# The first layer's opening by feature tiles: sums, modulation and float32 products of two projection chunks in one loop over k

## The chip, the cores and the metric

The kernel runs as one program on one core of a Trainium2 chip. The metric is the device time of one execution in microseconds, taken from the median of several runs. Engines are named as in the profile: PE is TensorE (its weight loads are PEld), DVE is VectorE, ACT is ScalarE, POOL is GpSimd, and SP issues nearly all transfers. The core has 16 DMA engines.

## The reference, cut to what matters

Two layers run one after the other over 256 tokens of 1,024 features. What the change touches is the beginning of the first layer: the adaLN sums of shift and scale, the modulated input `h`, and the first 1,024 of the 7,680 columns of the combined projection (`q_a` and `k_a`, the queries and keys of the differential attention, which are rotated afterwards).

```python
c_act = jax.nn.silu(c)
for l in range(DEPTH):
    mod = c_act @ ada_w[l] + ada_b[l]
    shift_m, scale_m, gate_m, shift_f, scale_f, gate_f = jnp.split(mod[:, None, :], 6, axis=-1)
    h = rms_norm(x, mix_norm_g[l]) * (1.0 + scale_m) + shift_m
    y = hybrid_mixer(h, w_in[l], ...)      # z = h @ w_in, three attentions, gates, w_out
    x = x + gate_m * y
    h = rms_norm(x, ffn_norm_g[l]) * (1.0 + scale_f) + shift_f
    x = x + gate_f * hier_moe(h, ...)      # 32 experts, all their weights are read
return rms_norm(x, final_norm_g)
```

## The kernel before, in words

**Layout.** Features lie on partitions in eight tiles k = 0 to 7 (`KD`), tokens along the free dimension, so the transposed input `xT` is 128 x 8 x 256. All weights are read once, in float32, into a pool of ten `pair` buffers of 2 MB; half a pair is a `slot` of 1 MB. The framework's scheduler puts the instructions of each engine into an order of its own; only what is wrapped in `keep_in_program_order` stays where it is written. Each engine then works strictly through its list. Of SP's transfers eight are under way at most: each waits for the landing of the one eight places ahead of it.

**Projection.** `mixer` treats `w_in` as 15 chunks of 512 columns. `load` brings a chunk in as two slots. `gemm` takes it in four pieces of two feature tiles. `split` (L302, L303) cuts each piece into a rounded part `whi` (ScalarE) and a rest `wlo` (VectorE), and the input is cut in the same way into `hi` and `lo`; three products in the one-pass format fp32r then stand for one float32 product. Chunks 0 and 1 (`rq` and `rk` in the table `SEGS`) take 96 matmuls of 256 columns each. What a chunk leaves in PSUM (`z`, buffers `acc`, four of them) is put off in `pending` and written out in the middle of the next chunk: `place` copies the rotated halves (L461, four ScalarE copies of 32 partitions), multiplies with cosine and sine (L462, L463, VectorE) and adds the two (L464, GpSimd).

**The opening.** `run` issues eight `ada_part` first: 1 MB of `ada_w` each, two dot products with the conditioning row `grb` each (`ada_sum`, L166, VectorE), all of shift (section 0) and then all of scale (section 1). `first_loads` stands behind the second of them and brings in `k1` (identity), the small columns and `x`. `mixer` then squares `x` for the norm (L218), transposes it (L233), and `modulated` makes 1/rms (`rstd`, `rsqrt`), spreads it over partitions through TensorE as `R`, and goes over k: split of a piece of chunk 0, scaling (L263), shift to `hi` on ScalarE (L265), rest to `lo` (L257). Every k needs the finished sums of all 16 tiles, because `ada_done` (L175, L181) works on whole columns.

**Filling.** The other adaLN sections are summed in between: `FILL[l][n]` says how many 1 MB pieces are taken up ahead of chunk n.

**After the mixer's projections** come the three attentions interleaved with the gate chunks, `w_proj`, `w_out`, then `moe`, which streams the experts' weights through the ten pairs. Layer 1 goes the same way.

Of the kernel before, what the change touches and what calls it, by code (L numbers as in the profile page):

```python
# [53 lines left out]
def bc(ap, at, n):  # L54

    a = [list(e) for e in ap.ap]
    a.insert(at, [0, n])
    return bass.AP(tensor=ap.tensor, offset=ap.offset, ap=a)


class Kernel:
# [56 lines left out]

    def first_loads(self):
        nc, io = self.nc, self.io  # L120
        nc.sync.dma_start(self.k1, io["k1"])
        for l in range(DEPTH):
            nc.sync.dma_start(self.gcol[l], self.io["g_col"][l])
            nc.sync.dma_start(self.mcol[l], self.io["ada_b"][l])
        nc.sync.dma_start(self.x, io["x"].rearrange("(p t) d -> p t d", t=2))
        tri = self.rwg.rearrange("p k n -> p (k n)")[:, :P]
        nc.sync.dma_start(tri, io["tri"])
        nc.vector.tensor_copy(self.tri, tri)
# [34 lines left out]
            self.ada_done(l, s)  # L163

    def ada_sum(self, w, to):
        self.nc.vector.tensor_tensor_reduce(w, w, self.grb, scale=1.0, scalar=0.0, op0=OP.mult, op1=OP.add,  # L166
                                            accum_out=to)

    FILL = (0, 1, 0, 3, 0, 2, 2, 3, 2, 2, 3, 2, 3, 0, 1), (0, 0, 2, 2, 2, 2, 2, 2, 1, 3, 0, 0, 0, 0, 0)
    MOVED = (2, 3, 4, 5)  # L170

    def ada_done(self, l, s):
# [71 lines left out]
    def modulated(self, l, w):  # L244
# [24 lines left out]
        low(KD - 1)  # L269
        return hi, lo, parts  # L270

    def to_hilo(self, src, done):
# [77 lines left out]
    def mixer(self, l, fill):  # L350
# [15 lines left out]
        w0 = load(0)  # L366
        M = self.xT.rearrange("p k n -> p (k n)")

        def take(n, of):
# [1 line left out]
            for b in tiles:  # L371
                nc.gpsimd.memset(b[:, 2047:2048], 0.0)
            return tiles
        G2, Q0, Q1, K0, K1, V0, V1, T0, T1 = take(9, "long")
        self.homes = [self.slot("parts"), self.slot("parts"), None, None]
        ga = []
        tok = [M[:, t * D:(t + 1) * D] for t in range(2)]
# [16 lines left out]
            return T[:, o + 512 * i:o + 512 * (i + 1)]  # L394
        self.work, self.junk = work, T0[:, 1536:1664]

        if l == 0:
            self.new_sums()
            for t in range(2):
                for half in range(2):  # L400
                    hs = slice(half * 512, (half + 1) * 512)
                    self.square(t, half, self.x[:, t, hs], (T0, T1)[t][:, hs])
            for c in range(4):
                self.raw_t(c)
        hi, lo, halves = self.modulated(l, [w0[k // 4][:, k % 4:k % 4 + 2] for k in range(0, KD, 2)])
# [10 lines left out]

        def chunk(n):
            w = load(n) if n else w0
            if n == 0:
                nc.sync.dma_start(self.rope, io["rope"])  # L420
            if n == 1 and l:
                self.conditioning()
            if n == 4:
                late_loads()
            for _ in range(self.FILL[l][n]):
                if fill:
                    fill.pop(0)()
            evac, prods = [], []
            for kind, c0, wd, dst in SEGS[n]:
                if wd == 512:  # L430
                    z = [self.acc(), self.acc()]
                    prods += self.wide(z)
                    evac += [lambda t=t, z=z, kind=kind, dst=dst:
                             nc.scalar.copy(vdst[kind][:, t, dst:dst + 512], z[t]) for t in range(2)]
                    continue
                z = self.acc()
                if kind in vdst:
                    prods += [(z[:, t * 256:(t + 1) * 256], False, t, slice(c0, c0 + 256), t == 0) for t in range(2)]
                    evac.append(lambda z=z, kind=kind, dst=dst: nc.scalar.copy(
                        vdst[kind][:, :, dst:dst + 256], z.rearrange("p (t n) -> p t n", t=2)))  # L440
                    continue
                prods += self.flipped(z, c0)
                if kind == "g":
                    evac.append(lambda z=z, dst=dst: nc.scalar.activation(ga[dst // 2], z, AF.Tanh, scale=0.5))
# [18 lines left out]
            nc.vector.tensor_mul(v(sh), v(sh), sin)  # L463
            nc.gpsimd.tensor_add(d, d, sh)  # L464

        for n in range(9):
            chunk(n)
        self.flush()
        self.diff_attention(l, qT, kT, va, tok)
# [536 lines left out]
    def run(self):  # L1006
        self.setup()
        ada = lambda l, s: [lambda h=h: self.ada_part(l, s, h) for h in range(4)]
        for i, f in enumerate(ada(0, 0) + ada(0, 1)):
            if i == 2:  # L1010
                self.first_loads()
            f()
        fill = [[f for l, s in parts for f in ada(l, s)] for parts in (
            [(0, s) for s in (2, 3, 4, 5)] + [(1, s) for s in range(6) if s not in self.MOVED],
            [(1, s) for s in self.MOVED])]
        for l in range(DEPTH):
            self.mixer(l, fill[l])
            self.moe(l)
        self.final()


def layout(inputs):
# [88 lines left out]
```

## Time and profile before

| what | value |
|---|---|
| median of 3 runs | 1509.85 us (1509.48 to 1510.61) |
| the profiled execution's own time | 1507.89 us |
| its span, first to last instruction | 1506.0 us |
| mean granted TensorE clock | 0.907 of full speed |
| first layer: mixer, then experts | up to about 340 us, then up to about 800 us |
| bytes moved | 544.43 MB, mean 362 GB/s |

To read it: the page gives busy times over the span and in 40 slices of 37.65 us; the tables by stretch give the same for any window; the timeline lists single instructions with the idle time ahead of them and what ended it. A float32 matmul of the program stands as two MATMUL rows in the trace, an fp32r matmul as one. A duration of a MATMUL contains its modelled way through the array, so the pace is read from the distance between starts.

### The profile page before, as it was taken

The page shows a single profiled execution, that of the slowest core. Times are in us where ns is not written, and L with a number is a line of the kernel's source. Part 1 is how long each engine was busy: PE and PEld are TensorE (multiplying, and loading weights), DVE is VectorE, ACT ScalarE, POOL GpSimd, SP SyncE. Part 2 cuts the span into 40 slices and gives each one's busy share as a digit, 9 for nine tenths or more (in the row PEclk, how much of TensorE's full clock was granted, in tenths as well). Part 3 has the DMA queues.
Part 4 walks back from the last instruction along what each step waited for, and adds up shares of the span by engine and source line. Part 5 has one row for each costly group of instructions (what it writes and reads, how often), then busy time and mean ns, then how long its engine had stood idle before and what let it go on. Part 6 is the DMA issues. An engine that isn't in the chain of part 4 may idle for free. (4 is left out here: it accounts for less than half of the span.)

```text
span 1506.0 us, 19652 instructions
## 1 busy us (share of the span) xinstructions
PE 1198.5 (80%) x8146; PEld 787.0 (52%) x8146; DVE 614.6 (41%) x1246; ACT 372.2 (25%) x664; POOL 57.5 (4%) x67
## 2 busy tenths in 40 slices
PE   2999998989877676676778999999787578577675
PEld 2898987874333132231358989889443133133132
DVE  6889974572121021110149997457322112022012
ACT  2765554350000000000046656544100000000001
POOL 0102000100000000000001110010000000000001
PEclk7999998899988897897999999999998888798898
DMA  9887971769999999999996965276999999999997
GB/s 373 351 348 279 380 293 57 298 254 390 427 428 427 427 427 428 429 427 428 424 416 280 390 276 221 113 284 247 365 426 429 426 430 426 427 429 427 429 428 296
DMA packets 53084, 544.43 MB, mean 362 GB/s; under 512 B 7168, under 2 KB 8192, under 8 KB 12160
## 3 DMA queue, kind: packets, MB, share of 16 engines
q1 hardware_dynamic: 52992, 543.13, 86.9%
q8 instruction: 66, 1.08, 0.3%
q14 instruction: 26, 0.21, 0.0%
HBM read 542.04 MB, written 1.06 MB: 361 GB/s over the span
## 5 line engine op out<-in xcount | busy, mean ns | idle before, releaser
L95 PE MATMUL acc<-rg,xg 128*32 128x512 f32 x2048 | 282.0, 694 | 115.6 <-DMA rg<-w 113.5
L95 PE MATMUL acc<-rg,b 128*32 128x512 f32 (+1 forms) x1152 | 153.0, 662 | 95.9 <-DMA rg<-w2g 69.2
L95 PEld LDWEIGHTS acc<-rg,xg 128*32 128x32 f32 x2048 | 68.6, 119 | 304.3 <-issue 295.1
L95 PE MATMUL acc<-hi,wlo 128*128 128x256 f32 x704 | 200.2, 289 | 7.9 <-DVE wlo L303 7.7
L95 PE MATMUL acc<-lo,whi 128*128 128x256 f32 x704 | 196.1, 284 | 0.0
L95 PE MATMUL acc<-hi,whi 128*128 128x256 f32 x704 | 191.4, 286 | 1.2 <-ACT whi L302 1.1
L303 DVE TENSOR_TENSOR wlo<-rg,whi 128x1024 fp32r<-128x1024 f32 x116 | 145.0, 1250 | 59.1 <-ACT whi L302 58.1
L813 DVE TENSOR_TENSOR b<-b,acc 128x512 f32<-128x512 f32 x16 | 11.0, 688 | 353.1 <-PE acc L95 353.1
L302 ACT CAST whi<-rg 128x1024 fp32r<-128x1024 f32 x116 | 121.5, 1047 | 107.4 <-PE acc L95 99.2
L95 PEld LDWEIGHTS acc<-hi,wlo 128*128 128x128 f32 x704 | 135.1, 192 | 15.3 <-DVE wlo L303 11.6
L95 PEld LDWEIGHTS acc<-rg,b 128*32 128x32 f32 x1152 | 33.9, 120 | 197.1 <-DMA rg<-w2g 105.1
L95 PEld LDWEIGHTS acc<-lo,whi 128*128 128x128 f32 x704 | 134.5, 192 | 1.4 <-issue 1.0
L95 PEld LDWEIGHTS misc<-b,xn 128*128 128x128 f32 x512 | 124.6, 334 | 16.9 <-issue 15.5
L95 PEld LDWEIGHTS acc<-hi,whi 128*128 128x128 f32 x704 | 131.0, 192 | 2.9 <-ACT whi L302 2.1
L95 PE MATMUL misc<-b,xn 128*128 128x128 f32 x512 | 125.6, 404 | 3.9 <-DVEq L918 2.0
L166 DVE CUSTOM_DVE_ANT_0 rg<-rg,grb 128x1024 f32<-128x1024 f32 x96 | 118.6, 1274 | 10.0 <-DMA rg<-ada_w 9.8
L812 ACT ACTIVATE b<-acc 128x512 f32<-128x512 f32 x16 | 9.6, 597 | 440.7 <-PE acc L95 440.7
L826 DVE TENSOR_TENSOR Y<-acc,grb 128x512 f32<-128x512 f32 x28 | 19.4, 692 | 228.2 <-PE acc L95 228.2
L793 DVE TENSOR_SCALAR xg<-misc,mcol 128x128 f32<-128x128 f32 x128 | 44.3, 405 | 106.5 <-PE misc L95 106.5
L806 ACT COPY b<-misc 128x256 f32<-128x256 f32 x16 | 6.0, 373 | 329.2 <-PE misc L805 329.2
L95 PE MATMUL acc<-hi,rg 128*128 128x256 f32 x384 | 74.6, 293 | 13.1 <-ACT hi L265 12.1
L95 PEld LDWEIGHTS acc<-hi,rg 128*128 128x128 f32 x384 | 62.7, 201 | 14.4 <-ACT hi L265 12.6
(168 smaller groups left out, 1437.0 us busy)
## 6 DMA issues: line engine op xcount, KB each, us to landing
rg<-w SPq DMA_DIRECT2D x128, 2048.0 KB, 39.1
rg<-w2g SPq DMA_DIRECT2D x56, 2048.0 KB, 38.9
rg<-w_in SPq DMA_DIRECT2D x56, 1024.0 KB, 9.8
rg<-ada_w SPq DMA_DIRECT2D x48, 1024.0 KB, 8.3
rg<-w2c SPq DMA_DIRECT2D x12, 1024.0 KB, 26.8
rg<-w_proj SPq DMA_DIRECT2D x8, 1024.0 KB, 7.1
rg<-w_out SPq DMA_DIRECT2D x8, 1024.0 KB, 5.8
rg<-w_in SPq DMA_DIRECT2D x8, 512.0 KB, 14.9
```

The lines of the kernel that those rows point to most:

```text
L95: return self.nc.tensor.matmul(out, lhsT, rhs, start=start, stop=stop, **kw)
L166: self.nc.vector.tensor_tensor_reduce(w, w, self.grb, scale=1.0, scalar=0.0, op0=OP.mult, op1=OP.add, accum_out=to)
L302: keep(nc.scalar.copy(whi, w))
L303: keep(nc.vector.tensor_sub(wlo, w, whi.bitcast(F32)))
L793: nc.vector.tensor_scalar(xg[:, k, :], p[:, kk * P:(kk + 1) * P], gf[:, k:k + 1], sf[:, k:k + 1], op0=OP.mult, op1=OP.add)
L806: nc.scalar.copy(ST, p[:, :256])
L812: nc.scalar.activation(a, h1, AF.Silu)
L813: nc.vector.tensor_mul(a, a, h3)
L826: nc.vector.tensor_mul(Y[:, hs], y[half], self.grb[:, hs])
```

## The change

The first layer gets functions of its own for loading and opening; the second layer keeps `modulated` and all nine chunks as they were.

- **`first_weights`** issues `c` (still in `setup`), `k1` and `x` first, and then for each k two 512 KB pieces of `ada_w` (shift and scale of this feature tile) and one 512 KB piece of a new host layout `w_first`, the rows of k of the first 1,024 columns of `w_in`. The small columns stand behind the pieces of k = 0.
- **`opening`** squares and transposes `x`, makes 1/rms, and loops over k: two sums, the addition of the bias column, (1 + scale) times the norm's weight, scaling by that and `R`, shift on ScalarE, all for one feature tile; then eight float32 matmuls of 256 columns into four `acc` buffers that stay open over all k. After every second k the tile pair is cut into `hi` and `lo` for the chunks behind it.
- **Chunks 0 and 1** are therefore not split and not passed to `gemm`; all four `z` are handed to `place` at the end of the loop. `mixer` goes on with chunk 2.
- **`FILL`** of layer 0 puts one piece ahead of chunk 2 that stood ahead of chunk 1. `rope` is issued ahead of the opening.

```diff
+    FILL = (0, 0, 1, 3, 0, 2, 2, 3, 2, 2, 3, 2, 3, 0, 1), ...     # layer 0 was (0, 1, 0, 3, ...)
+    def first_weights(self):
+        nc.sync.dma_start(self.k1, io["k1"])
+        nc.sync.dma_start(self.x, io["x"].rearrange("(p t) d -> p t d", t=2))
+        for k in range(KD):
+            aw.append(self.slot("ada").rearrange("p (s n) -> p s n", s=2))
+            for s in range(2):
+                src = io["ada_w"][0, s, k // 2].rearrange("p (m n) -> p m n", m=2)
+                nc.sync.dma_start(aw[k][:, s, :], src[:, k % 2, :])
+            if k == 0:
+                self.first_loads()
+            if k % 2 == 0:
+                w.append(self.slot().rearrange("p (k n) -> p k n", k=2))
+            src = io["w_first"][k // 2].rearrange("p (k n) -> p k n", k=2)
+            nc.sync.dma_start(w[-1][:, k % 2, :], src[:, k % 2, :])
+    def opening(self, aw, w, done):
+        for k in range(KD):
+            for s in range(2):
+                keep(self.ada_sum(aw[k][:, s, :], sums[:, k, s:s + 1]))
+            keep(V.tensor_add(m[:, 0:2, k], m[:, 0:2, k], sums[:, k, :]))
+            keep(V.scalar_tensor_tensor(m[:, 1, k:k + 1], m[:, 1, k:k + 1], 1.0, self.gcol[0][:, 0, k:k + 1],
+                                        op0=OP.add, op1=OP.mult))
+            keep(V.scalar_tensor_tensor(xT[:, k, :], xT[:, k, :], m[:, 1, k:k + 1], R, op0=OP.mult, op1=OP.mult))
+            keep(nc.scalar.activation(xT[:, k, :], xT[:, k, :], AF.Identity, bias=m[:, 0, k:k + 1]))
+            for i in range(8):
+                self.mm(z[i // 2][:, i % 2 * 256:(i % 2 + 1) * 256], w[k // 2][:, k % 2, i * P:(i + 1) * P], xT[:, k, :],
+                        k == 0 and i % 2 == 0, k == KD - 1, skip_group_check=True)
+            if k % 2:
+                nc.scalar.copy(hi[:, k - 1:k + 1, :], xT[:, k - 1:k + 1, :])
+                V.tensor_sub(lo[:, k - 1:k + 1, :], xT[:, k - 1:k + 1, :], hi[:, k - 1:k + 1, :].bitcast(F32))
+        for i in range(4):
+            done(i, z[i])
...
-        for n in range(9):
+        nc.sync.dma_start(self.rope, io["rope"])
+        if l == 0:
+            hi, lo = self.opening(*firsts, lambda i, z: place(z, "rk", (*qT2[:2], *kT2[:2])[i]))
+        else:
+            hi, lo, halves = self.modulated(l, [w0[k // 4][:, k % 4:k % 4 + 2] for k in range(0, KD, 2)])
+        for n in range(0 if l else 2, 9):
             chunk(n)
```

VectorE, the end of the sums and the first feature tiles, before (`sums` holds the dot products, `mcol_74` the columns of shift and scale, `rg` any buffer of the pool):

```order
L166 ISA sums 128x1
L175 TENSOR_TENSOR mcol_74<-mcol_74,sums 128x8
L303 TENSOR_TENSOR rg<-rg 128x1024
L181 SCALAR_TENSOR_TENSOR mcol_74<-mcol_74,gcol_76 128x8
L263 SCALAR_TENSOR_TENSOR rg<-rg,mcol_74,acc 128x256 x2
L257 SCALAR_TENSOR_TENSOR lo<-rg,mcol_74,hi 128x256 x2
```

The same engine now, from the second sum of an odd k to the first sum of the next k (`first` holds the dot products):

```order
L164 ISA first 128x1
L312 TENSOR_TENSOR mcol_74<-mcol_74,first 128x2
L313 SCALAR_TENSOR_TENSOR mcol_74<-mcol_74,gcol_76 128x1
L315 SCALAR_TENSOR_TENSOR rg<-rg,mcol_74,misc 128x256
L322 TENSOR_TENSOR lo<-rg,hi 128x512
L164 ISA rg,first<-rg,grb 128x1024
```

The column work came down from once per section to once per k, the splits are gone, and `lo` of two tiles stands directly behind the scaling of the odd tile and ahead of the next sums.

ScalarE, around the output of chunks 0 and 1, before (`whi_432` is the last piece of chunk 1, `whi_493` and `whi_523` belong to chunk 2):

```order
L302 CAST rg<-rg 128x1024
L461 COPY rg<-acc 32x512 x8
L302 CAST whi_432<-rg 128x1024
L302 CAST rg<-rg 128x1024
L302 CAST whi_493<-rg 128x1024
L302 CAST rg<-rg 128x1024
L461 COPY rg<-acc 32x512 x8
```

The same engine now, from the last feature tiles on (`whi_381` is the third piece of chunk 2):

```order
L316 ACTIVATE rg<-rg,mcol_74 128x256 x2
L321 CAST hi<-rg 128x512
L138 ACT_TABLE_LOAD
L138 ACTIVATE lpe<-lps 128x2
L509 COPY rg<-acc 32x512 x16
L357 CAST rg<-rg 128x1024 x2
L357 CAST whi_381<-rg 128x1024
```

All 16 copies of the four outputs now stand together ahead of the first split of chunk 2; before, eight of them stood ahead of it by one split and eight behind several.

TensorE at the border of chunks 1 and 2, before:

```order
L95 MATMUL acc<-lo,whi_390 128x256
L95 MATMUL acc<-rg,hi 128x512 x2
L95 MATMUL acc<-rg,lo 128x512
L95 MATMUL acc<-hi,whi_432 128x256 x2
L95 MATMUL acc<-hi,wlo_433 128x256
```

The same engine now (`misc<-rg` of 256 columns is the score product of the first attention head, which needs the placed outputs):

```order
L95 MATMUL misc<-k_72,rsq 128x128 x2
L95 MATMUL acc<-rg 128x256 x64
L95 MATMUL misc<-rg 128x256 x4
L95 MATMUL acc<-rg,hi 128x512 x3
L95 MATMUL acc<-rg,lo 128x512
```

The 64 float32 matmuls stand in one row, the scores of the first head moved from behind most of chunk 2 to ahead of it, and the last piece of chunk 1 no longer mixes with chunk 2.

## Rows read from the trace of the kernel before

**Rows 1.** The page: what the DMA moved per second, in 40 slices of 37.65 us.

```profile
GB/s 373 351 348 279 380 293 57 298 254 390 427 428 427 427 427 428 429 427 428 424 416 280 390 276 221 113 284 247 365 426 429 426 430 426 427 429 427 429 428 296
```

**Rows 2.** Busy time by stretch of the first layer's mixer: length, then us busy and (instructions) of PE, PEld, DVE, ACT, POOL, then granted clock, DMA share, GB/s.

```profile
20.00:30.00 10.00, 1.19 (x4) 0.92 (x4) 9.96 (x21) 0.08 (x1) 0.00 (x0) 0.56 1.01 416
30.00:40.00 10.00, 5.96 (x34) 5.96 (x35) 8.46 (x17) 4.66 (x7) 0.00 (x0) 0.59 0.95 375
...
60.00:100.00 40.00, 39.26 (x290) 36.78 (x289) 34.55 (x50) 24.51 (x39) 4.00 (x3) 1.00 0.87 351
...
130.00:136.00 6.00, 3.90 (x20) 3.27 (x20) 6.00 (x6) 1.05 (x1) 3.40 (x2) 0.82 0.30 96
136.00:200.00 64.00, 61.13 (x441) 56.16 (x440) 61.47 (x134) 33.29 (x68) 2.13 (x1) 0.99 0.86 351
```

**Rows 3.** Timeline of all engines in the opening: start, duration, engine, line, operation, and in brackets the idle time ahead with what ended it.

```profile
5.28 1.06 ACT L117 ACTIVATE grb<-grb 128x1024 f32<-128x1024 f32 x1 [3.24 <-DMA grb<-c]
...
13.47 0.63 ACT L218 ACTIVATE rg<-x 128x512 f32<-128x512 f32 x1 [7.14 <-DMA x<-x]
...
16.14 0.16 DVE L223 TENSOR_REDUCE rstd<-ssq 128x2 f32<-128x6 f32 x1 [2.25 <-ACT rg L218]
...
31.29 0.08 DVE L166 DVE_READ_ACCUMULATOR2_ANT sums<- 128x1 f32 x1
31.41 0.17 DVE L175 TENSOR_TENSOR mcol<-mcol,sums 128x8 f32<-128x8 f32 x1
...
32.63 0.16 DVE L181 SCALAR_TENSOR_TENSOR mcol<-mcol,gcol 128x8 f32<-128x8 f32 x1
32.91 0.87 DVE L263 SCALAR_TENSOR_TENSOR rg<-rg,mcol,acc 128x256 f32<-128x256 f32 x2
33.48 0.91 ACT L265 ACTIVATE hi<-rg,mcol 128x256 fp32r<-128x256 f32 x2 [2.51 <-DVE rg L263]
...
34.04 1.22 PE L95 MATMUL acc<-hi,rg 128*128 128x256 f32 x4 [10.49 <-ACT hi L265]
```

**Rows 4.** The chain that ended last, in order of time: the same norm chain at the end of the program, where nothing lies between its steps (start, duration, what); its first row and the last two steps.

```profile
1498.44 0.17 DVE rstd L223
...
1499.89 0.17 DVE rsq L208
...
1500.09 0.17 DVE rsq L209
```

**Rows 5.** Timeline of PE: the pace of fp32r matmuls of 256 columns, the start of chunk 2, and two stalls with the scores of the first head between them.

```profile
39.92 0.40 PE L95 MATMUL acc<-hi,rg 128*128 128x256 f32 x2
40.16 0.28 PE L95 MATMUL acc<-lo,rg 128*128 128x256 f32 x1
...
57.65 0.63 PE L95 MATMUL acc<-rg,hi 128*128 128x512 f32 x2
...
61.70 0.39 PE L95 MATMUL acc<-hi,wlo 128*128 128x256 f32 x1 [0.44 <-DVE wlo L303]
...
73.10 1.13 PE L95 MATMUL misc<-rg 64*128 64x256 f32 x8
74.53 0.50 PE L95 MATMUL acc<-wlo,hi 128*128 128x512 f32 x1 [0.30 <-DVE wlo L303]
```

**Rows 6.** Groups of matmuls in the first 345 us, float32 with a full 128 x 128 weight tile: shape, count, busy us, mean ns of one, idle before.

```profile
L95 PE MATMUL misc<-rg 128*128 128x128 f32 x32 | 4.2, 274 | 0.0
```

**Rows 7.** Granted clock around the start of the matmuls, behind a gap of PE, and late in the attentions; columns as in Rows 2.

```profile
36.00:38.00 2.00, 2.00 (x11) 2.00 (x11) 1.76 (x4) 0.94 (x3) 0.00 (x0) 0.50 0.97 382
38.00:40.00 2.00, 2.00 (x18) 2.00 (x17) 1.55 (x3) 0.91 (x1) 0.00 (x0) 0.94 1.09 423
...
134.00:137.00 3.00, 3.00 (x16) 3.00 (x16) 3.00 (x4) 0.00 (x0) 0.60 (x1) 0.50 0.78 270
...
274.00:277.00 3.00, 3.00 (x19) 2.29 (x18) 0.69 (x1) 1.11 (x2) 0.00 (x0) 0.50 0.99 426
```

**Rows 8.** Timeline of ACT: a table load, the copies of `place` and the split behind them.

```profile
42.52 1.28 ACT L140 ACT_TABLE_LOAD   x1
...
52.24 4.71 ACT L461 COPY rg<-acc 32x512 f32<-32x512 f32 x8
56.98 1.05 ACT L302 CAST whi<-rg 128x1024 fp32r<-128x1024 f32 x1
```

**Rows 9.** Timeline of DVE around the first `place`, a sum, a split and the next sum.

```profile
55.23 0.68 DVE L463 TENSOR_TENSOR rg<-rg 128x512 f32<-128x512 f32 x1
56.99 0.69 DVE L462 TENSOR_TENSOR rg<-acc,rg 128x512 f32<-128x512 f32 x1 [1.08 <-ACT rg L461]
57.59 0.68 DVE L463 TENSOR_TENSOR rg<-rg 128x512 f32<-128x512 f32 x1
58.19 1.22 DVE L166 CUSTOM_DVE_ANT_0 rg<-rg,grb 128x1024 f32<-128x1024 f32 x1
...
59.34 2.31 DVE L303 TENSOR_TENSOR wlo<-rg,whi 128x1024 fp32r<-128x1024 f32 x1
61.57 1.21 DVE L166 CUSTOM_DVE_ANT_0 rg<-rg,grb 128x1024 f32<-128x1024 f32 x1
```

**Rows 10.** Timeline of POOL: the additions of `place`.

```profile
56.06 1.29 POOL L464 TENSOR_TENSOR rg<-rg 128x512 f32<-128x512 f32 x1 [54.86 <-DVE rg L463]
58.42 2.14 POOL L464 TENSOR_TENSOR rg<-rg 128x512 f32<-128x512 f32 x1 [1.06 <-DVE rg L463]
```

More of the change, by code (lines that the diff above doesn't have):

```diff
@@ L120, in first_loads @@
         nc, io = self.nc, self.io
-        nc.sync.dma_start(self.k1, io["k1"])
         for l in range(DEPTH):
@@ L124, in first_loads @@
             nc.sync.dma_start(self.mcol[l], self.io["ada_b"][l])
-        nc.sync.dma_start(self.x, io["x"].rearrange("(p t) d -> p t d", t=2))
         tri = self.rwg.rearrange("p k n -> p (k n)")[:, :P]
@@ L165, in ada_sum @@
     def ada_sum(self, w, to):
-        self.nc.vector.tensor_tensor_reduce(w, w, self.grb, scale=1.0, scalar=0.0, op0=OP.mult, op1=OP.add,
-                                            accum_out=to)
-    FILL = (0, 1, 0, 3, 0, 2, 2, 3, 2, 2, 3, 2, 3, 0, 1), (0, 0, 2, 2, 2, 2, 2, 2, 1, 3, 0, 0, 0, 0, 0)
+        return self.nc.vector.tensor_tensor_reduce(w, w, self.grb, scale=1.0, scalar=0.0, op0=OP.mult, op1=OP.add,
+                                                   accum_out=to)
+    FILL = (0, 0, 1, 3, 0, 2, 2, 3, 2, 2, 3, 2, 3, 0, 1), (0, 0, 2, 2, 2, 2, 2, 2, 1, 3, 0, 0, 0, 0, 0)
     MOVED = (2, 3, 4, 5)
@@ L270, in modulated @@
         return hi, lo, parts
+    def first_weights(self):
+        nc, io = self.nc, self.io
+        nc.sync.dma_start(self.k1, io["k1"])
+        nc.sync.dma_start(self.x, io["x"].rearrange("(p t) d -> p t d", t=2))
+        aw, w = [], []
+        for k in range(KD):
[9 more added lines that the diff above has]
+            nc.sync.dma_start(w[-1][:, k % 2, :], src[:, k % 2, :])
+        return aw, w
@@ new lines, in opening @@
+    def opening(self, aw, w, done):
+        nc = self.nc
+        V, m, xT = nc.vector, self.mcol[0], self.xT
+        for t in range(2):
+            for half in range(2):
+                self.square(t, half, self.x[:, t, half * 512:(half + 1) * 512], self.misc())
+        for c in range(4):
+            self.raw_t(c)
+        r = self.rstd()
+        self.rest()
+        R = self.misc()[:, :256]
+        for t in range(2):
+            self.mm(R[:, t * P:(t + 1) * P], bc(r[:, t], 1, P), self.ident, t == 0, t == 1, skip_group_check=True)
+        hi, lo = self.hilo()
+        sums = self.cst.tile([P, KD, 2], F32, name="first")
+        z = [self.acc() for _ in range(4)]
+        keep = self.tc.keep_in_program_order
+        for k in range(KD):
[14 more added lines that the diff above has]
+            done(i, z[i])
+        return hi, lo
@@ L365, in load @@
             return w
-        w0 = load(0)
         M = self.xT.rearrange("p k n -> p (k n)")
@@ L373, in take @@
             return tiles
-        G2, Q0, Q1, K0, K1, V0, V1, T0, T1 = take(9, "long")
+        G2, = take(1, "long")
+        if l == 0:
+            self.new_sums()
+            firsts = self.first_weights()
+        else:
+            w0 = load(0)
+        Q0, Q1, K0, K1, V0, V1, T0, T1 = take(8, "long")
         self.homes = [self.slot("parts"), self.slot("parts"), None, None]
@@ L395, in mixer @@
         self.work, self.junk = work, T0[:, 1536:1664]
[L397 to L405, printed above, removed]
         def late_loads():
@@ L418, in chunk @@
             w = load(n) if n else w0
-            if n == 0:
-                nc.sync.dma_start(self.rope, io["rope"])
             if n == 1 and l:
@@ L464, in place @@
             nc.gpsimd.tensor_add(d, d, sh)
-        for n in range(9):
+        nc.sync.dma_start(self.rope, io["rope"])
+        if l == 0:
+            hi, lo = self.opening(*firsts, lambda i, z: place(z, "rk", (*qT2[:2], *kT2[:2])[i]))
+        else:
+            hi, lo, halves = self.modulated(l, [w0[k // 4][:, k % 4:k % 4 + 2] for k in range(0, KD, 2)])
+        for n in range(0 if l else 2, 9):
             chunk(n)
@@ L1008, in run @@
         ada = lambda l, s: [lambda h=h: self.ada_part(l, s, h) for h in range(4)]
[L1009 to L1012, printed above, removed]
         fill = [[f for l, s in parts for f in ada(l, s)] for parts in (
@@ L1032, in layout @@
     a["ada_w"] = aw.reshape(DEPTH, 6, 4, 2, P, D).swapaxes(3, 4).reshape(DEPTH, 6, 4, P, 2 * D)
+    a["w_first"] = g["w_in"][0, :, :2 * 512].reshape(4, 2, P, 2 * 512).swapaxes(1, 2).reshape(4, P, 4 * 512)
     a["w_in"] = g["w_in"].reshape(DEPTH, 2, 4, P, 15, 512).transpose(0, 4, 1, 3, 2, 5).reshape(DEPTH, 15, 2, P, 2048)
```

## Prediction

> **What bounds the kernel now.** I read the page first, then busy time by stretch, then the timeline of the opening. Over the whole span the DMA is the largest load: the slices of the two expert phases stand at 424 to 430 GB/s [rows 1]. The first layer's mixer is not of that kind. From 60 to 100 and 136 to 200 us PE is busy 39.3 of 40 us and 61.1 of 64, and VectorE lies just behind it (34.6 of 40, 61.5 of 64) [rows 2]. Before 60 us it is otherwise: PE has 1.2 us of work between 20 and 30 us, while VectorE works through the sums (9.96 of 10 us) and the DMA runs at 416 GB/s [rows 2]; the first projection matmul starts at 34.04 us, after ScalarE's first `hi`, which waited for the last sum at 31.29 us [rows 3]. The change works on this idle opening. As PE and VectorE are full behind it, and the experts' stream starts when the mixer frees its buffers, I count an earlier state of both engines at chunk 2 fully to the end.
>
> **What stands against what.** For PE, the mark is the time at which chunk 2 would start if all earlier work were done and PE never waited again. Before, chunk 2 begins at 57.65 us, but a quarter of chunk 1 (24 matmuls at 0.12 us, as 39.92 to 40.16 us holds two: 2.9 us), two stalls (0.44 and 0.30 us) and the first head's scores (1.13 us) lie behind that point [rows 5] and, in the new order, ahead of it. 57.65 + 2.9 + 0.7 + 1.1 gives a mark of 62.4 us.
>
> **The change, step by step.** *Start.* `c` landed at about 5.2 us (its Silu starts at 5.28) [rows 3]; `k1` and `x`, 1.13 MB, now follow it directly; at 416 GB/s [rows 2] they land at 8.0 us. From the landing of `x` to the row sums took 13.47 to 16.14, 2.67 us [rows 3]; the norm chain without sums in between took 1498.44 to 1500.26, 1.82 us [rows 4]. The first new sum thus starts at 12.5 us.
>
> *One feature tile on VectorE.* Two sums at 1.15 us (58.19 to 59.34) [rows 9]; 0.12 us to the column addition (31.29 to 31.41) [rows 3]; 0.20 us to the next small step (1499.89 to 1500.09) [rows 4]; 0.28 us to the scaling (32.63 to 32.91) [rows 3]. That is 2.90 us to the start of the scaling, and with its 0.43 us (0.87 for two) 3.33 us. On an odd tile VectorE then stands before `lo`: ScalarE's shift starts 0.57 us after the scaling and takes 0.45 [rows 3], its cast of 512 columns 0.55 (an estimate: half of 1.05 [rows 8]), `lo` itself 0.60 (56.99 to 57.59 for 512 columns) [rows 9]. The odd tile costs 2.90 + 2.2 = 5.1 us, a pair 8.4 us. The scaling of the last tile starts at 12.5 + 3 x 8.4 + 3.33 + 2.90 = 44.0 us. PE can take a tile 1.13 us after its scaling starts (32.91 to 34.04) [rows 3]: the first at 16.5, the seventh at 41.8, the last at 45.1 us.
>
> *PE's float32 work.* The 64 products are 128 rows of the trace. No row before has this shape. From below, an fp32r matmul of 256 columns takes 0.12 us; from above, the score rows, two side by side, take 1.13 / 4 = 0.28 us a pair [rows 5]. The nearest row has the same full weight tile and 128 columns: 4.2 / 32 = 0.131 us [rows 6]; twice that less a little fixed cost is 0.24 us, which I take. A tile then costs 16 x 0.24 = 3.8 us, less than VectorE's 4.2. The clock was granted at half speed for the first 4 us of matmuls (34 to 38) and then full [rows 7]; the same loss at 16.5 us is made up long before the end. PE finishes the seventh tile at 45.6, the last at 49.5 us, the first output bank at 46.6. At 0.12 us nothing changes, since VectorE sets the pace; at 0.28 PE needs 16.5 + 128 x 0.28 + 2.0 = 54.3 us and everything behind comes 4 us later.
>
> *The output.* ScalarE is done with the last shift and cast at 45.6 us, has a table load of 1.28 us next, and then, without a break, 16 copies at 4.71 / 8 = 0.59 us [rows 8]: 46.9 to 56.3 us. This is where the early start is given back: before, eight of these copies lay beside matmuls of chunk 1 and eight beside chunk 2; now PE has nothing else to do. Chunk 2's first cast ends at 57.4. VectorE could begin its half of the split there, but GpSimd's last addition starts 0.83 us after VectorE's last multiplication (55.23 to 56.06 [rows 9, 10]), at 57.2, and takes 1.29; a split beside such an addition took 2.31 us instead of about 1.15, and ended just after it [rows 9, 10]. So the first `wlo` is there at 58.5 + 1.15 = 59.7 us. The scores, which now stand ahead of chunk 2 on PE, need the third output: copied at 54.0, added at 56.1, so they run from 56.2 to at most 58.5 at half clock, ahead of that.
>
> *The clock once more.* PE is idle from 49.5 to 56.2 us. PE worked only 3.9 of 6 us from 130 to 136, and the granted clock was 0.50 from 134 to 137 [rows 2, 7]. I charge 4 us at half speed from 59.7 on, 2.0 us. PE's mark is 61.7 against 62.4: 0.7 us won.
>
> *VectorE.* Eight splits of 1.15 us are gone (9.2 us), and most of that is spent on waiting for `lo` (three times 1.6 us, and once at the end) and for copies. At 61.57 us before [rows 9] it had done chunk 1, one split of chunk 2 and three sums of filling (3.45 us), not the two places of chunk 1 (four steps of 0.60, 2.4 us). After, at 59.7, it has done one split of chunk 2 and all places, no filling. That is 1.9 - 3.45 + 2.4 = 0.85 us won, and up to 1.95 us if one of the two additions that before still lay ahead would again have held a split up by 1.1 us.
>
> *Transfers.* By 42.2 us, when VectorE takes the last scale tile, 13.9 MB must have landed, 1.7 of them by 8.0: 12.2 MB in 34.2 us, 357 GB/s. At 416 they are there at 37.3 us, so the DMA stays hidden by 5 us. Then 2.2 MB of small loads and chunk 2's 2.1 MB land near 49 us, before 57.4. SP next waits for PE to release `w_first` at 49.5, with a filling piece and chunk 3 queued behind that wait; 4.2 MB later, at about 62 us, chunk 3 is there, ten us before PE wants it. Layer 1 keeps its work and is costed at nothing; PE and VectorE cover its changed order of issues.
>
> **The sum.** Between 0.7 and 1.95 us are won; I take 1.2. The profiled execution took 1507.89 us, 1.96 under the median, and its span 1506.0; the difference is carried to the median: 1509.85 - 1.2 = 1508.7 us. About 0.2%, 3 us, is what a measurement of this kernel can tell from no change, so this is no change.
>
> **Rivals.**
> - *VectorE's lead pays more.* In 130 to 136 us VectorE was full and PE worked 3.9 of 6 us, with the clock at 0.50 up to 137 [rows 2, 7]: 2.1 us of idle time and 1.5 us of clock. A lead of 2 us there could remove both: 1509.85 - 1.95 - 3.6 = 1504.3. For it: VectorE is as full as PE up to 200 us. Against: VectorE's order changes there as well.
> - *The small transfers become the bound* (the other side). The 1 MB pieces of `ada_w` became 512 KB pieces, with eight transfers under way at most. Below 357 GB/s the last tile waits; at 300 GB/s it would come at 8.0 + 40.7 = 48.7 instead of 42.2: 1515.2. For it: the stretch with four 512 KB pieces among its transfers shows 375 GB/s, near the threshold [rows 2]. Against: that stretch also holds small loads. The Trainium skill, page "DMA: Bandwidth & Descriptors", section "Measured (HBM→SBUF, 128 partitions, SWDGE, issued from GpSimd)", asks for batches of at least 1 MiB for three quarters of the peak, which speaks against this change. Its figure for 1 MB, 341 GB/s, would be an estimate of 43.8 us for the landing, 1.6 us late, and 1510.3; the trace's 416 GB/s does not agree with that figure.
> - *PE stays at half clock*, in the loop or after the gap, as at 274 to 277 us, where PE was full and the clock still at 0.50 [rows 7]. In the loop: 128 x 0.48 us from 16.5 ends at 78, the last copies, split and restart bring the mark to 85.7, 23.3 us behind: 1533. Against: 34 to 40 us shows the clock rise under steady matmuls, and with 7.7 us a tile PE would be steady.
> - *The new order costs something later:* one more stall like that of 130 to 136, 3.6 us: 1512.3.
>
> **How the numbers follow.** No change as summed 0.49; VectorE's lead 0.30; small transfers 0.08; half clock 0.06; order or PE at 0.28 us a row (1513) 0.07. Faster 0.30, the same 0.49, slower 0.21. The range leaves out the half clock, most of the small transfers' price and the ends: 1503.8 to 1513.8.
>
> **What would show it.** In the new profile: the first sum near 12.5 us, pairs of tiles every 8.4 us, PE's loop rows 0.24 us apart, ScalarE's 16 copies from 47 to 56 us, PE idle from 49.5 to 56, chunk 2 in earnest at about 60 us with the clock at 0.50. Wrong would be a VectorE that waits for `ada_w` in the loop, a loop at half clock, or a chunk 2 that starts well before 59 us.

## The result, and the profile after

The changed kernel takes 1500.45 us (median of 5 executions, 1499.06 to 1502.79) beside 1509.48 us before (5 executions, 1506.92 to 1510.61): ratio 0.9945, 95% interval 0.9932 to 0.9958. It is 9.0 us faster, outside the predicted range; no change was predicted. Its profiled execution took 1502.16 us with a span of 1500.4 us. Lines behind the opening have moved by 48 to 55: L302 and L303 are L357 and L358 now, L444 is L492, L493 is L546, L659 is L712.

**The opening came as predicted.** Timeline of the changed kernel, VectorE's first feature tile to PE's first product, then the output and the restart (start, duration, engine, line, idle ahead in brackets); it answers [rows 3, 5, 8, 9 and 10].

```profile
12.40 1.22 DVE L164 CUSTOM_DVE_ANT_0 rg<-rg,grb 128x1024 f32<-128x1024 f32 x1
...
15.31 0.48 DVE L315 SCALAR_TENSOR_TENSOR rg<-rg,mcol,misc 128x256 f32<-128x256 f32 x1 [0.15 <-DVE mcol L313]
...
16.39 1.22 PE L95 MATMUL acc<-rg 128*128 128x256 f32 x2 [2.57 <-ACT rg L316]
...
46.66 9.43 ACT L509 COPY rg<-acc 32x512 f32<-32x512 f32 x16
46.82 1.67 PE L95 MATMUL acc<-rg 128*128 128x256 f32 x7
...
56.51 2.08 PE L95 MATMUL misc<-rg 64*128 64x256 f32 x8 [8.01 <-POOL rg L512]
...
57.33 3.44 DVE L358 TENSOR_TENSOR rg<-rg 128x1024 fp32r<-128x1024 f32 x2
57.56 2.14 POOL L512 TENSOR_TENSOR rg<-rg 128x512 f32<-128x512 f32 x1 [1.10 <-DVE rg L511]
...
58.52 1.65 PE L95 MATMUL acc<-rg,hi 128*128 128x512 f32 x3
```

The first sum starts at 12.40 us (predicted 12.5), PE ends its loop at 46.82 + 1.67 = 48.5 (49.5), the 16 copies run from 46.66 to 56.1 (46.9 to 56.3), and PE idles 8.01 us until the scores. Busy time by stretch, columns as in [rows 2]; the first five rows answer to the five there, the last three give the clock around the restart:

```profile
20.00:30.00 10.00, 10.00 (x49) 8.72 (x48) 8.35 (x17) 1.82 (x4) 0.00 (x0) 1.00 1.03 413
30.00:40.00 10.00, 8.87 (x41) 7.33 (x39) 8.53 (x20) 1.64 (x3) 0.00 (x0) 1.00 1.02 404
60.00:100.00 40.00, 39.71 (x288) 37.63 (x287) 35.18 (x54) 20.10 (x32) 1.90 (x1) 1.00 0.93 370
130.00:136.00 6.00, 4.78 (x28) 3.58 (x27) 6.00 (x12) 5.07 (x8) 0.00 (x0) 1.00 0.47 168
136.00:200.00 64.00, 61.03 (x449) 55.91 (x448) 61.72 (x141) 30.86 (x67) 3.27 (x1) 1.00 0.88 352
...
50.00:56.00 6.00, 0.00 (x0) 0.00 (x0) 2.90 (x5) 5.86 (x11) 3.33 (x3) 0.78 0.95 382
58.00:60.00 2.00, 2.00 (x8) 1.20 (x5) 2.00 (x2) 2.00 (x3) 1.69 (x1) 0.50 0.98 416
60.00:62.00 2.00, 2.00 (x10) 1.67 (x9) 2.00 (x3) 0.00 (x1) 0.00 (x0) 0.94 1.05 442
```

PE begins chunk 2 at 58.52 us, as the first split on VectorE ends, and the clock is back from 0.50 (1.2 GHz) just after 60 us. The two splits in the row of 3.44 us are not alike (shortest, middle and longest duration, then first and last start):

```profile
L358 DVE TENSOR_TENSOR rg<-rg x2: 1217/1764/2310, 57.3 to 58.5; 128x1024 fp32r<-128x1024 f32 x2
```

The first started ahead of GpSimd's addition (57.56) and took its usual 1.22 us, to 58.55; the second, beside the addition, took 2.31. Chunk 3's first matmul starts at 70.31. Chunk 2's 48 matmuls at 0.227 us (24 in 5.44 us up to there) take 10.9, so PE's mark is 59.4 against 62.4: 3.0 us won where 0.7 were predicted. The output of chunk 2 is copied at 72.92, before at 76.45: 3.5 us.

**The rest of the gain is 200 us later.** I cut the remainder of the first layer's mixer at two events: the last gate evacuation (the last `tanh`, L444 before) and the first gated product of `w_proj` (L493 before). What lies between them I call the tail. By stretch, chunk 2's copy to the last gate and then the tail, first before:

```profile
76.50:248.70 172.20, 167.19 (x1269) 155.94 (x1267) 142.70 (x285) 94.47 (x172) 11.24 (x8) 0.99 0.74 296
248.70:282.90 34.20, 27.72 (x145) 22.07 (x146) 11.09 (x25) 12.22 (x26) 0.00 (x0) 0.60 0.35 140
```

and after:

```profile
72.90:245.90 173.00, 167.76 (x1277) 155.49 (x1277) 144.77 (x284) 95.03 (x170) 13.21 (x8) 1.00 0.75 292
245.90:273.30 27.40, 22.95 (x141) 18.64 (x142) 10.39 (x23) 11.00 (x23) 0.00 (x0) 0.75 0.47 186
```

To the last gate 172.2 and 173.0 us: the lead goes from 3.6 to 2.8. The tail takes 34.2 and 27.4 us: 6.8 more, 9.6 in all, and 8.9 of them still stand at the end of the first layer's experts (756.0 us before, 747.1 after). PE's busy time by the mean clock is 27.7 x 0.60 = 16.6 us and 23.0 x 0.75 = 17.2 us: the same work within 4% (an estimate from these rows). What differs is idle time (6.5 and 4.5 us) and the clock (11.1 and 5.7 us).

Of the 8.9 us, 5.6 are left at the end of these two traces (1506.0 less 1500.4), though the medians differ by 9.0. A part of the loss is in the second layer, in the same stretch from its last gate to its `w_proj`, first before and then after:

```profile
997.10:1006.90 9.80, 8.34 (x72) 7.59 (x73) 5.02 (x6) 5.51 (x10) 0.00 (x0) 1.00 0.98 417
988.80:1000.15 11.35, 9.89 (x72) 8.98 (x73) 5.09 (x6) 5.62 (x10) 0.00 (x0) 0.85 1.00 424
```

The same 72 rows of PE take 1.6 us longer at a lower clock. Of the 14 traces of this document, ten have the 9.8 us at 1.00 and four some 11.3 us at 0.85 (after, a_late, a_e2f, b_nodil). With one trace of each kernel, it stays open whether this goes with the kernel or with the execution; the end of a single trace can be off by it.

The tail is the end of the dilated attention: pairs of heads, each a chain of scores, row minimum (VectorE), exponential (ScalarE), scaling, transposes and products. Its timeline before, rows of the chain:

```profile
248.72 0.59 ACT L444 ACTIVATE rg<-acc 128x512 f32<-128x512 f32 x1
...
252.30 1.09 PE L560 MATMUL misc<-k,rg 128*128 128x128 f32 x4 [3.64 <-DVE rg L663]
253.32 6.59 PE L95 MATMUL misc<-rg 128*64 128x128 f32 x28
...
256.05 0.69 DVE L659 CUSTOM_DVE_ANT_0 rg<-misc,rg 128x512 f32<-128x512 f32 x1 [3.89 <-PE misc L95]
...
266.11 0.69 DVE L659 CUSTOM_DVE_ANT_0 rg<-misc,rg 128x512 f32<-128x512 f32 x1 [3.89 <-PE misc L95]
...
282.88 1.35 DVE L493 SCALAR_TENSOR_TENSOR rg<-rg,acc 128x512 f32<-128x512 f32 x2
```

and after:

```profile
245.88 0.59 ACT L492 ACTIVATE rg<-acc 128x512 f32<-128x512 f32 x1
...
247.36 0.69 DVE L712 CUSTOM_DVE_ANT_0 rg<-misc,rg 128x512 f32<-128x512 f32 x1 [0.66 <-PE misc L95]
...
253.25 0.63 PE L613 MATMUL misc<-k,rg 128*128 128x128 f32 x4 [2.20 <-DVE rg L716]
...
255.72 0.69 DVE L712 CUSTOM_DVE_ANT_0 rg<-misc,rg 128x512 f32<-128x512 f32 x1 [2.62 <-PE misc L95]
...
273.26 1.35 DVE L546 SCALAR_TENSOR_TENSOR rg<-rg,acc 128x512 f32<-128x512 f32 x2
```

What moved there shows in VectorE's list. Each `.` is one split, `|` the last split of a chunk, `o` half the output of a head of the differential attention, `N` and `D` a row minimum of the neighbourhood and of the dilated attention, `P` the first product of `w_proj`; first chunk 13, then 14, then the splits of `w_proj`:

```
before   .NNNN.oo..|   NNNN..D.D.|   .DD.DDDD.P
after    NNoo..NN.NN.| .D.D..|       DD.D.DDD.P
```

The neighbourhood attention now ends ahead of the last split of chunk 13, one split sooner, and the dilated attention begins one split sooner in chunk 14. Before, PE runs out of work at 248.7 and waits 3.64 us for the chain; from 250 us on its clock is granted at 0.50, and a pair then takes 10.06 us (256.05 to 266.11), of which PE's 28 float32 rows take 6.59. After, the same wait is 2.20 us, the pair from 247.36 to 255.72 takes 8.36 us, and the clock is at 0.50 only later and for a shorter time.

### The profile page after: what moved, and what is told of

Its sections match the earlier page's. It is cut to its first block, busy times and chain, and to the rows that moved or that the text cites. A ratio compares the mean times of both kernels' runs of the same rounds, so it can differ in the third digit from the quotient of the medians.

```text
span 1500.4 us, 19517 instructions
## 1 busy us (share of the span) xinstructions
PE 1207.3 (80%) x8082; PEld 787.2 (52%) x8082; DVE 607.7 (41%) x1247; ACT 367.4 (24%) x660; POOL 59.4 (4%) x67
## 5 line engine op out<-in xcount | busy, mean ns | idle before, releaser
L95 PE MATMUL acc<-hi,wlo 128*128 128x256 f32 x672 | 191.7, 289 | 4.9 <-DVE wlo L358 4.7
L95 PE MATMUL acc<-lo,whi 128*128 128x256 f32 x672 | 188.1, 285 | 0.0
L95 PE MATMUL acc<-hi,whi 128*128 128x256 f32 x672 | 184.1, 287 | 0.9 <-ACT whi L357 0.9
L358 DVE TENSOR_TENSOR wlo<-rg,whi 128x1024 fp32r<-128x1024 f32 x112 | 139.2, 1243 | 59.3 <-ACT whi L357 55.8
L357 ACT CAST whi<-rg 128x1024 fp32r<-128x1024 f32 x112 | 117.3, 1048 | 105.1 <-PE acc L95 90.2
L95 PEld LDWEIGHTS acc<-hi,wlo 128*128 128x128 f32 x672 | 129.2, 192 | 10.5 <-DVE wlo L358 8.0
L95 PEld LDWEIGHTS acc<-lo,whi 128*128 128x128 f32 x672 | 128.6, 192 | 1.7 <-issue 1.4
L95 PEld LDWEIGHTS acc<-hi,whi 128*128 128x128 f32 x672 | 125.6, 193 | 2.9 <-ACT whi L357 1.5
L95 PE MATMUL misc<-rg 64*128 64x256 f32 (+4 forms) x416 | 66.8, 352 | 10.3 <-POOL rg L512 8.0
L95 PE MATMUL misc<-Y,b 128*128 128x512 f32 (+1 forms) x144 | 62.2, 571 | 4.9 <-DVE Y L819 4.9
```

Of the source, the lines that this page charges most:

```text
L95: return self.nc.tensor.matmul(out, lhsT, rhs, start=start, stop=stop, **kw)
L357: keep(nc.scalar.copy(whi, w))
L358: keep(nc.vector.tensor_sub(wlo, w, whi.bitcast(F32)))
```

## The experiments

Two theories. **T1:** the opening's lead is everything, and what follows carries it on. **T2:** the opening gives about 3 us, and about 6 us come from the tail, because the scheduler ordered attentions and gate chunks anew. Each experiment has the kernel of before beside it on the same chip; its medians there were 1507.84 to 1508.90 us. One table for all, from the traces (us: copy of chunk 2, last gate, first product of `w_proj`; then the tail, PE's MATMUL rows in it, its mean clock, and the median of all executions). Tails with 141 to 145 rows hold the same work; each matmul added in the warm kernels counts two rows.

| kernel | chunk 2 | last gate | w_proj | tail | rows | clock | median |
|---|---|---|---|---|---|---|---|
| before | 76.5 | 248.7 | 282.9 | 34.2 | 145 | 0.60 | 1509.48 |
| after | 72.9 | 245.9 | 273.3 | 27.4 | 141 | 0.75 | 1500.45 |
| b_fill | 77.9 | 250.5 | 284.7 | 34.2 | 145 | 0.60 | 1510.32 |
| a_early1 | 74.4 | 251.4 | 285.1 | 33.7 | 145 | 0.65 | 1510.59 |
| a_late | 75.5 | 255.7 | 280.4 | 24.7 | 109 | 0.65 | 1603.71 |
| a_late2 | 76.2 | 249.9 | 277.3 | 27.4 | 142 | 0.75 | 1503.30 |
| a_fillb | 72.8 | 250.3 | 274.1 | 23.8 | 142 | 0.86 | 1499.73 |
| a_e1f | 69.4 | 252.1 | 276.9 | 24.8 | 108 | 0.66 | 1500.74 |
| a_e2f | 69.3 | 253.1 | 267.2 | 14.1 | 105 | 1.00 | 1498.43 |
| b_warm3 | 76.8 | 249.0 | 277.4 | 28.4 | 163 | 1.00 | 1504.40 |
| a_warm3 | 72.9 | 247.2 | 273.3 | 26.1 | 159 | 1.00 | 1500.21 |
| a_warm6 | 73.4 | 246.3 | 271.1 | 24.8 | 154 | 1.00 | 1498.22 |
| b_nodil | 76.3 | 243.0 | 251.0 | 8.0 | 45 | 0.79 | 1479.79 |
| a_nodil | 73.9 | 240.8 | 249.0 | 8.2 | 45 | 0.79 | 1474.94 |

**1. The pair without a tail.** Both kernels without layer 0's dilated attention:

```diff
-        self.dil_attention(l, qT, kT, vd, oT[1])
+        if l:
+            self.dil_attention(l, qT, kT, vd, oT[1])
+        else:
+            nc.gpsimd.memset(oT[1], 0.0)
```

> The kernel before without the dilated attention of layer 0 (its output is set to zero; everything else stays). It is half of a pair with a_nodil: in both, the first layer's tail of dependent VectorE, ScalarE and PE steps is gone, and the gate chunks end the attention. Theory T2 (3 us of the 9 come from PE's earlier chunk 2, about 6 from a shorter tail of the dilated attention): the changed kernel leads this pair by 2 to 4.5 us. Rival T1 (all 9 us come from the opening and are carried through whatever follows): by 8 to 10 us. By itself this kernel should lose 20 to 25 us against before if the tail alone (250 to 273 us) falls away.

> The changed kernel without the dilated attention of layer 0 (output set to zero). Beside b_nodil: T2 2 to 4.5 us less than b_nodil, T1 8 to 10 us less. Last gate evacuation in both: about 3 us earlier here by either theory.

b_nodil took 1479.79 us (ratio to before 0.9808, 0.9794 to 0.9821), a_nodil 1474.94 (0.9779, 0.9766 to 0.9793): 4.9 us apart by medians and 4.4 by ratios (give or take 3), at the upper edge of what T2 said and half of T1's. b_nodil lost 28.1 us against before, more than the 20 to 25 expected. In the traces the last gate comes 2.2 us earlier and `w_proj` 2.0, where the full kernels differ by 9.6: at `w_proj`, 7.6 of the 9.6 us need the dilated attention. The rest of the 4.9 arises behind `w_proj` (in the traces the lead is 5.6 us at the second layer's last gate), and no run shows why.

**2. An earlier start with the old tail, and the filling alone.** In a_early1 the casts of chunk 2 are kept ahead of the last twelve copies; `NOW` is 1, and `keep` stands on these copies and casts.

```diff
-            done(i, z[i])
+            if i < NOW: done(i, z[i])
+            else: self.pending.append(lambda i=i: done(i, z[i]))
```

> The changed kernel, but the casts of chunk 2's first weights stand on ScalarE behind the 4 copies of the first projection output instead of behind all 16, so PE starts chunk 2 some 4 us sooner; the scheduler then orders the dilated attention of layer 0 against the gate chunks word for word as in the kernel before. T1 (an earlier PE is carried through): 1495 to 1498.5, faster than the change. T2 (the tail's gain goes with the order): PE leads by 5 to 7 us at the last gate chunk and no more at the end of the attention, total 1502 to 1505, slower than the change although PE starts earlier.

> The kernel before with the change's table of filling places alone (the one filling place of chunk 1 goes to chunk 2); the order of the dilated attention against the gate chunks stays that of before. T1 and T2: within 2 us of before (1508 to 1511). Rival T3 (the filling table, not the opening, makes the gain): 1500 to 1504.

a_early1: 1510.59 us, ratio 1.0016 (1.0007 to 1.0025), no faster than before. It did not do what it was made for. A filling sum that waited for its DMA now stood ahead of the first split on VectorE, and chunk 2 began later, not sooner; its timeline:

```profile
57.30 1.23 DVE L164 CUSTOM_DVE_ANT_0 rg<-rg,grb 128x1024 f32<-128x1024 f32 x1 [4.78 <-DMA rg<-ada_w]
...
60.87 0.80 PE L95 MATMUL acc<-rg,hi 128*128 128x512 f32 x1 [6.97 <-DVE rg L363]
```

Both totals expected were missed; both rest on a start of chunk 2 ahead of the changed kernel's, and it did not come. Two things remain: with the order of before (the engines' lists agree with those of before from 144 us on) the tail is again 33.7 us, as T2 has it, and a lead of 2.1 us at chunk 2 had turned into 2.7 us behind at the last gate. b_fill, 1510.32 us (1.0014, 1.0005 to 1.0023), 2.5 us above the kernel beside it, has the tail of before to a tenth, and the 1.8 us that it is behind at the last gate are there at `w_proj`: the filling table alone gives nothing, and T3 falls.

**3. The change with a later opening.** a_late repeats the first sum; a_late2 instead passes twice over the first tile on VectorE.

```diff
+            for _ in range(0 if k else 2):
+                keep(V.tensor_scalar(aw[0], aw[0], 1.0, None, op0=OP.mult))
```

> The changed kernel with three more sums on VectorE ahead of the first feature tile (the first shift sum made four times, about 3.5 us), so its whole opening is 3 to 3.5 us later; the scheduler thereby orders the first layer's rest anew: four of the eight rows L659 of the dilated attention now stand on VectorE among the splits of the last gate chunk, where the changed kernel has two. T1 (the opening's lead is what pays): 1503 to 1505. T2 (the tail of the dilated attention pays, PE's lead only what remains of it): PE no more than 1.5 us ahead of before at the last gate chunk, the tail shorter than in the changed kernel, 1496 to 1501, no slower than the changed kernel though it begins later.

> The changed kernel with two passes over the first tile of ada_w (times 1.0) on VectorE ahead of the first sum, about 1.9 us each, so that the opening is 3.5 to 4 us later and PE's lead at chunk 2 is gone; the order of the last gate chunks and of the attentions is word for word that of the changed kernel. T1 (the opening's lead is all): as before, 1507 to 1509. T2 (the order of the attentions against the gate chunks makes two thirds): PE level with before at the end of chunk 2, the tail still about 27 us and not 34, 1502 to 1505.

a_late took 1603.71 us (1.0629, 1.0615 to 1.0644), and both theories' totals were missed. It tells nothing by its total: a sum writes its products over its tile, so the repeats changed the modulation and with it the data of all that follows. Then the branch for experts with too many tokens (`overflow_block`) ran, at 422.6 to 468.4 us in its trace and in no other trace; between the 25th and the 33rd load of the experts' `w13` 144.7 us pass, before 49.5, which is 95 of the 96 us by which the second layer's `w_proj` is late. Its last gate is 7.0 us behind before, and `w_proj` 2.5 us ahead. a_late2 took 1503.30 us (0.9970, 0.9959 to 0.9981), in T2's range and outside T1's. Its lists of the engines agree with the changed kernel's from 203 us on. Its first sum came 2.9 us later than there (3.5 to 4 were expected), its lead was gone at chunk 2 (76.2 against 76.5) and negative at the last gate, and yet `w_proj` came 5.6 us ahead of before, all of it from the tail:

```profile
76.20:249.90 173.70, 168.66 (x1286) 156.91 (x1285) 144.59 (x288) 94.87 (x169) 12.17 (x8) 1.00 0.74 294
249.90:277.30 27.40, 22.94 (x142) 18.35 (x142) 10.27 (x23) 10.95 (x23) 0.00 (x0) 0.75 0.44 175
```

Of these, 5.2 us still stand in the span (1506.0 less 1500.8), and by the medians it is 5.6 (1508.90 less 1503.30). This is the split of the 9.0 us: about 6 from the tail, about 3 from the opening (1503.30 less 1500.45 is 2.9). By the ratios, each taken against its own neighbour, it is 4.5 and 3.8 of 8.3 us, the difference give or take 2.6; both parts are there, their sizes are known to 2 or 3 us.

**4. Other orders.** a_fillb is the change with before's `FILL`; a_e1f and a_e2f are a_early1 with `NOW` 1 and 2 and the filling piece of chunk 2 moved to chunk 3.

> The changed kernel with the filling table of before (the one place of chunk 2 then belongs to chunk 1, which this opening doesn't call, so the piece comes later). The neighbourhood attention stands half a chunk behind its place in the changed kernel, two rows of the dilated attention among the splits of chunk 14 as there. T1: 1499 to 1502. T2: the chain of the attentions is less far ahead, 1502 to 1506.

> As a_e2f, but with the casts behind 4 of the 16 copies; four rows of the dilated attention stand among the splits of chunk 14 and four behind them. PE's chunk 2 some 4 us sooner than in the changed kernel. T1: 1495 to 1498. T2: 1491 to 1497.

> The changed kernel with the casts of chunk 2's first weights behind 8 of the 16 copies, and with chunk 2's one filling place moved to chunk 3, so that no filling sum stands ahead of chunk 2's splits on VectorE (as one did in a_early1). PE's chunk 2 should start some 3 us sooner than in the changed kernel. The order puts four rows of the dilated attention ahead of the last two splits of chunk 14 and two more among them. T1: 1496 to 1498.5 (the change less the 3 us). T2: 1489 to 1495 (those 3 us and a tail shorter by two to four rows).

a_fillb: 1499.73 us (0.9938, 0.9925 to 0.9952), within T1's range. T2 as written missed, since I had judged by how far the chain stands ahead. By that measure it is worse than the change, with the last gate even 1.6 us behind before; but the tail is 23.8 us, at a clock of 0.86:

```profile
250.30:274.10 23.80, 20.20 (x142) 16.71 (x142) 10.20 (x23) 10.95 (x23) 0.00 (x0) 0.86 0.54 217
```

a_e1f: 1500.74 us (0.9955, 0.9941 to 0.9969), slower than either theory said. Its 7.1 us of lead at chunk 2 were gone at the last gate (252.1), and its tail was at 0.66. a_e2f: 1498.43 us (0.9934, 0.9920 to 0.9948), within T1's range and outside T2's, though the trace has what T2 asked for: a tail of 14.1 us at clock 1.00, and `w_proj` 15.7 us ahead of before. (The tails of a_e1f and a_e2f are short in part because they hold less, 108 and 105 rows; the rest of that work lies ahead of a later last gate.) Of the 15.7, 12.7 reached the end in the profiled execution, which was the fastest of the five at 1495.05, and 1.6 were lost in the second layer's stretch of 11.3 us; the median shows 9.7 (1508.14 less 1498.43). Where the others lost the rest is open. In all of these, the lead at chunk 2 and at the last gate are no guide to the end; `w_proj`'s start is a better one.

**5. The clock in the tail, by itself.** Useless matmuls where PE idles between two heads; in b_warm3 and a_warm3 in the last three pairs, in a_warm6 in the last two:

```diff
                     pts.append(self.pt(lambda i: E[:, i * P:(i + 1) * P], 4, "PD", keep))
+                    for _ in range(3 if not l and hp + tq and len(pts) == 1 else 0):
+                        keep(self.mm(self.adap(), self.ident, self.x[:, 0, :512], True, True))
```

> The kernel before with three added float32 matmuls of 512 columns (identity by x, result thrown away) on PE between the transposes of the first and of the second head in each of the last three pairs of the dilated attention of layer 0, where PE otherwise idles 1.4 to 3.6 us. The order of everything else stays. If the granted clock fell in the tail because PE idled there (part of T2: most of the difference between the tails is the clock), the clock stays near 1.00, the stretch from the last gate evacuation to the first product of the projection shrinks from 34.2 to 26 to 30 us, and the kernel takes 1501 to 1505. If the clock stays at 0.50 whatever PE does in the gaps, the added work costs 1.5 to 3.5 us in each pair: 1513 to 1518.

> The changed kernel with the same added matmuls. Its tail is at half clock for a shorter time, so there is less to win: if the clock can be held, 27.4 becomes 24 to 27 us and the kernel 1497 to 1500; if not, 1504 to 1509. If the clock in the tail is what the two kernels differ by, b_warm3 comes within 2 to 5 us of a_warm3, where the kernels as they are differ by 9.

> The changed kernel with the three added matmuls in the last two pairs alone, so that none of them stands ahead of the last gate chunk (in a_warm3 three did, and the last gate evacuation came 1.3 us later); order otherwise word for word that of the changed kernel. PE then has work between 251 and 253 us, where it idled 2.2 us ahead of the fall of the clock. If that idle time is what lets the clock fall: clock 1.00 to the first product of the projection, a stretch of 23 to 25 us instead of 27.4, 1496 to 1499. If the clock falls all the same: 1501 to 1505.

b_warm3 took 1504.40 us (0.9974, 0.9964 to 0.9984), as expected if the clock can be held: nine added matmuls made the kernel of before 4.5 us faster. Its tail, then those of a_warm3 and a_warm6:

```profile
249.00:277.40 28.40, 26.79 (x163) 17.45 (x162) 10.87 (x24) 11.96 (x26) 0.00 (x0) 1.00 0.41 162
```

```profile
247.20:273.30 26.10, 25.02 (x159) 17.20 (x159) 10.21 (x22) 10.79 (x23) 0.00 (x0) 1.00 0.44 172
246.30:271.10 24.80, 23.35 (x154) 16.36 (x154) 10.22 (x23) 10.82 (x23) 0.00 (x0) 1.00 0.47 184
```

In b_warm3 the clock stays at 1.00, and 5.8 of the 34.2 us are gone; the lists of all engines are otherwise those of before, word for word. The execution profiled, 1502.65 us, is among the faster of nine that go up to 1506.53, and whether the clock held in the others is not known. a_warm3: 1500.21 us (0.9949, 0.9936 to 0.9963), 0.2 us above what was expected and no better than the change. Of the three matmuls of its first pair one stands ahead of the last gate products (243.96 us) and two right behind them (246.61), and the last gate comes 1.3 us later; the expectation of a_warm6 has all three ahead of it. a_warm6 without those three: 1498.22 us (0.9928, 0.9914 to 0.9941), 2.2 us under the change by medians, with intervals that overlap.

With the clock held on both sides, the tail of b_warm3 is 2.3 us longer than that of a_warm3 and 3.6 us longer than that of a_warm6, where the kernels as they are differ by 6.8; the medians are 4.2 and 6.2 us apart instead of 9.0. So about half to two thirds of the difference between the tails is the clock (3.2 or 4.5 of 6.8 us), the rest is the order at full clock. PE's idle time between the heads is what let the clock fall: with work there, it did not fall in the tail of either kernel. The Trainium skill, page "TensorE: Matmul & The Clock Gate", section "Loop structure matters more than you think", says that the loop nest decides whether matmuls stay warm, that is at the fast clock; its bad case is a long wait for DMA between matmuls. In this case's traces the loops of the tail are the same in all kernels and PE waits for VectorE; the order in which the scheduler laid them out was enough for a mean clock of 0.60 in one kernel and 0.75 or 0.86 in others.

## Why the prediction was wrong

- **Opening on VectorE, ACT and PE's loop: right.** 12.40 us for 12.5, pairs of tiles every 8.3 us for 8.4, the loop's end at 48.5 for 49.5, copies to 56.1 for 56.3. A row of float32 takes 0.22 us (the last 32 rows start at 41.32 to 48.12 us) where 0.24 was taken between bounds of 0.12 and 0.28.
- **Transfers: right.** VectorE never waited for `ada_w` in the loop; the DMA moved 404 to 413 GB/s in 512 KB pieces. The rival of the small transfers is out.
- **The restart of chunk 2: mechanism right in part, size wrong.** The collision of split and GpSimd addition is there, but it hit the second split: the first had started ahead of the addition and was there at 58.55, not 59.7. I also charged 4 us at half clock from 59.7 on, 2.0 us lost; PE began at 58.52, and the clock was back soon after 60, so some 0.9 us were lost (an estimate from the rows of 58 to 62 us). Together that is the 2.3 us by which the mark was better than predicted: it won 3.0 us, not 0.7. This term is the opening's share, about 3 us.
- **The step that failed:** "I count an earlier state of both engines at chunk 2 fully to the end." The argument was that PE and VectorE are full behind it. I had looked at 60 to 100 and 136 to 200 us, where they are, and left 247 to 277 out of account, where neither is, though the last row of [rows 7] shows PE there at a clock of 0.50. There the order decides, and the change gave the scheduler a new problem: its order left a tail of 27.4 us instead of 34.2. a_late2 shows this order's tail without the opening's lead, a_early1 and b_fill show the old order's tail (33.7 and 34.2 us) with other openings, and b_warm3 beside a_warm3 and a_warm6 shows that about half to two thirds of the difference is the clock. With the restart put right, the sum would have been 1509.85 - 3.0 = 1506.9 us, inside the range; the tail is what took the time out of it.
- **The rivals.** VectorE's lead at 130 to 136 us paid a little: PE is busy 4.78 of 6 us instead of 3.90, at clock 1.00 instead of 0.82; yet the last gate is only 2.8 us earlier, so it adds nothing to the opening's share. VectorE's own term (0.85 to 1.95 us) was not measured by itself. Half clock in the loop did not come. "The new order costs something later" had the right place in general and the wrong sign.

Open: why the scheduler's orders differ as they do, why the second layer's stretch takes 9.8 us in some traces and 11.3 in others, and what else takes back a part of a lead at `w_proj` from one execution to the next.

## What to carry to other kernels

Where a scheduler orders the engines, an edit at the beginning reorders the whole, so compare the order at every later place where a chain of small steps runs out of independent work, not only where the edit is. Look there for the granted clock: with gaps of 1.4 to 3.6 us of PE in such a chain, it ran at 1.2 GHz for most of its 34.2 us here, and some matmuls without use in those gaps got 5.8 us back. Such matmuls must not stand ahead of other work: the three in the pair that still overlaps the last gate chunk took their gain away in a_warm3. A lead is worth about what is left of it at the next point where all engines meet, here the start of `w_proj`, and at times less (a_e2f: 15.7 us there, 9.7 by the median).

## What the hardware showed unexpectedly

- Added work made a kernel faster: nine float32 matmuls of 512 columns, 4.5 us less (0.9974, 0.9964 to 0.9984), with the clock in the tail at 1.00 instead of 0.60 in the execution profiled.
- In the tail of before the clock stayed at 0.50 from 250 to about 277 us, although rows in between show PE without a gap (one of several 5 us windows):

```profile
255.00:260.00 5.00, 5.00 (x26) 4.03 (x25) 1.40 (x5) 1.08 (x3) 0.00 (x0) 0.50 0.00 0
```

- Transfers of 512 KB, eight under way, ran at 404 to 413 GB/s from 20 to 40 us. The Trainium skill, page "DMA: Bandwidth & Descriptors", section "Measured (HBM→SBUF, 128 partitions, SWDGE, issued from GpSimd)", asks for at least 1 MiB for three quarters of the peak, from transfers issued by GpSimd; these are issued by SP and reach 94% of the 430 GB/s of the expert phases [rows 1], so the trace shows that the rule does not carry over to this queue.
